# Root mean squares spread by four transposes, decay exponents formed on ACT by a relu with bias, key-value latents issued ahead of the index keys, SBUF padding of 72 instead of 88 words

## The chip, the cores and the metric

The kernel runs on one core of a Trainium2 chip. The metric is device microseconds (us) of one execution, from the median of three runs. TensorE (PE in the views) does the matrix products, VectorE (DVE) and ScalarE (ACT) the elementwise work, GpSimd (POOL) some more of it, and SyncE (SP) issues every DMA. Each engine takes its instructions in one fixed order and waits where an operand or a buffer is not ready.

## The reference, cut to what matters

One layer of a hybrid encoder on 512 tokens of 1024 channels: a layer norm, a mixing block with two branches, a layer norm, a feed-forward block with a convolution, a layer norm. The parts that the change touches:

```
# state-space branch, 32 heads in pairs, chunks of 64 tokens in the reference
a_cum = cumsum(dt * A)                        # per head
seg   = a_cum[..., :, None] - a_cum[..., None, :]
decay = exp(where(causal, seg, -inf))         # <= 1: seg is <= 0 where causal
y_diag = einsum(cb * decay, X)
v = v * rsqrt(mean(v * v over 512 channels) + eps)     # 4 groups

# attention branch
ckv   = ckv * rsqrt(mean(ckv * ckv) + eps) * kv_norm_g # 256 latent channels
k_idx = layernorm(k_idx)                               # index keys
score = sum_h relu(q_idx . k_idx) * w_idx              # selects 128 keys per query
```

The kernel works in chunks of 128 tokens. Everything is float32; the large products are split into a high and a low part in the type float32r and done as three products (high x high, low x high, high x low).

## The kernel before, in words

Activations lie with channels on the 128 partitions and 512 tokens along a row. A weight block of 128 x 1024 comes by one DMA into `wraw` (4 buffers), ACT copies it to the high part `whi` (L190), DVE subtracts to get the low part `wlo` (L191, 3 buffers each), and PE runs 24 matmuls with it (`proj`, L228, recorded at L217) into one of three PSUM accumulators `pacc`. A projection of 512 tokens thus is 24 matmuls of 512 columns.

The stages in order of time: input norm and small projections (to about 56 us), `decays` (L471), `index_keys` (L428), `latents` (L513), `scores` (L451), then the state-space part (to about 485 us): for each of four groups, `ssd_in` projects and convolves six blocks, and `ssd_core` handles one pair of heads, 16 times. In `ssd_core` the tile `G` is read back from memory (a row of cumulative decays spread over all partitions, L590), the exponent is formed by 8 DVE instructions (L623: subtract the token's own value, then the minimum with 0), ACT takes the exponential (L625), DVE multiplies by the masked products (L626), and PE uses it (L633). `ssd_norm` and `latents` call `rms_bcast` (L254): it sums squares by PE into a column per token (L259), takes the inverse root (DVE, POOL), writes it on a diagonal `dg` (DVE, L263) and spreads it over all partitions by one float32 product of 512 columns with ones (L266). After that come attention (485 to 667 us), the merge of both branches (`yahi`, `yalo` against `w_br_att`, to 709), the output projection (to 757), the feed-forward up-projection (`h1hi`, `h1lo`, to 1000) and down-projection (tiles `f`, `fw`, `fx`, `fy`, at L241).

Up to 485 us the order of instructions on each engine is made by a list scheduler from the order of the code and its own estimates of duration; from there on the order of PE is written out by hand or follows the code. Tiles live in pools. The left-hand pools (`cst`, `wrw`, `whl`, `keep`, `h1T`, `f` and others) grow from low addresses; `pad` and then `wk` are taken from the high end of a partition's memory:

```
pad = E(tc.tile_pool(name="pad", bufs=1, side="right"))
pad.tile([P, PAD], F32, name="pad")
wk = E(tc.tile_pool(name="wk", bufs=1, side="right"))
```

Nothing reads `pad`; it only moves `wk`. With 88 words `wk` begins at byte 116,352 of a partition, a multiple of 128, and so do its large tiles (`yhi`, `ylo`, `yahi`, `yalo`, `fw`, `fx`, `fy`, `wh`, `mhi`, `qi`, `G` and more). With 72 words it begins at 116,416, 64 bytes past a multiple of 128. The left-hand tiles that PE reads (`whi` and `wlo` from 24,768, `hhi` and `hlo` from 65,728, `h1hi` and `h1lo` from 49,344, the tiles `f` from 82,112, `ident` at 3,136) all begin 64 bytes past a multiple of 128.

Of the kernel before, what the change touches and what calls it, by code (L numbers as in the profile page):

```python
# [11 lines left out]
AF = mybir.ActivationFunctionType  # L12
OP = mybir.AluOpType
# [3 lines left out]
P = 128  # L17
T = 512
NT = T // P
# [17 lines left out]
OUT_STEPS = (0, 0, 0, 2, 4)  # L37
UNITS_A = [n / 18 for n in (0, 1, 1, 4, 2)]
UNITS_B = [n / 18 for n in (1, 2, 2, 5)]
PAD = 88  # L40
NOSYNC = mybir.DependencyInfo(mybir.DependencyClass.NoSync, mybir.DependencyReason.DATA)

VECS = [("ln_in_g", KD), ("ln_in_b", KD), ("kv_g", 2), ("conv_w", 96), ("conv_b", 24), ("norm_g", 16),
# [16 lines left out]
def tok(i):  # L60
    return slice(i * P, (i + 1) * P)
# [11 lines left out]
def block_kernel(ctx, tc, A, out):  # L73
    nc = tc.nc
# [15 lines left out]
    def wt(tag, shape, name, dtype=F32):  # L90
        return wk.tile(shape, dtype, name=name, tag=tag, bufs=BUFS[tag])
# [9 lines left out]
    def ct(shape, name, dtype=F32):  # L101
        return cst.tile(shape, dtype, name=name, tag=name)
# [22 lines left out]
    def flat(t):  # L125
        return t.rearrange("p a b -> p (a b)")
# [21 lines left out]
    ones = ct([P, P], "ones")  # L148
    nc.gpsimd.memset(ones, 1.0)
    ident = ct([P, P], "ident")  # L150
# [103 lines left out]
    def rms_bcast(sqs, n):  # L254

        s4 = ps("a")
        for i in range(NT):
            for j, sq in enumerate(sqs):
                nc.tensor.matmul(s4[:, i:i + 1], sq[:, tok(i)], ones[:, 0:1],  # L259
                                 start=j == 0, stop=j == len(sqs) - 1)  # L260
        r = rsqrt_small(s4[:, :NT], 1.0 / n, EPS, NT)
        dg = wt("m2", [P, NT, P], "dg")
        nc.vector.tensor_tensor(dg, ident[:, None, :].to_broadcast([P, NT, P]),  # L263
                                r[:, :, None].to_broadcast([P, NT, P]), OP.mult)
        rb = ps("b")
        nc.tensor.matmul(rb, ones, flat(dg), start=True, stop=True)  # L266
        return rb

    def stack_parts(even, odd, p, scale, cols):
# [27 lines left out]
    dt, dts, acT, cd = [kp.tile(SH, F32, name=n, tag=n) for n in ("dt", "dts", "acT", "cd")]  # L297
# [14 lines left out]
    V, S, G = "vector", "scalar", "gpsimd"  # L312
# [158 lines left out]
    def decays():  # L471
        dt4 = wt("m2", [P, 4, NT, NH], "dt4")
        u, e, s, s2 = [dt4[:, c] for c in range(4)]
        a = sp1[:, :NT * NH].rearrange("p (a b) -> p a b", a=NT)
        nc.vector.tensor_tensor(u, smt[:, :, 64:96], row["dt_bias"][:, None, :].to_broadcast(SH), OP.add)
        nc.vector.scalar_tensor_tensor(e, u, -1.0, u, OP.mult, OP.max)
        nc.scalar.activation(e, e, AF.Exp, scale=-1.0)
        nc.vector.tensor_scalar(s, e, 2.0, None, OP.add)
        nc.vector.reciprocal(s, s)
        nc.vector.tensor_tensor(s, s, e, OP.mult)  # L480
        nc.vector.tensor_tensor(s2, s, s, OP.mult)
        nc.vector.tensor_scalar(e, s2, 1.0 / 15.0, None, OP.mult)
        for c in (13, 11, 9, 7, 5, 3):
            nc.vector.scalar_tensor_tensor(e, e, 1.0 / c, s2, OP.add, OP.mult)
        nc.vector.scalar_tensor_tensor(e, e, 1.0, s, OP.add, OP.mult)
        nc.vector.tensor_scalar(u, u, 0.0, None, OP.max)
        nc.vector.scalar_tensor_tensor(dt, e, 2.0, u, OP.mult, OP.add)
        eA = sp1[:, 128:160]
        with tc.issue_after(last_pow[0].ins):
            nc.gpsimd.tensor_tensor(eA, e_t, row["A_log"], OP.pow)  # L490
        nc.vector.scalar_tensor_tensor(a, dt, -1.0, eA[:, None, :].to_broadcast(SH), OP.mult, OP.mult)
        ar = wt("m2", [NH, T], "ar")
        p = ps("c")
        for c in range(NT):
            nc.tensor.matmul(p[:NH, tok(c)], a[:, c], upper, start=True, stop=True)
        nc.scalar.activation(ar, p[:NH], AF.Copy)
        nc.sync.dma_start(ac_d, ar)
        ear = wt("m2", [NH, T], "ear")
        nc.scalar.activation(ear, ar, AF.Exp)
        nc.sync.dma_start(ea_d, ear)  # L500
        p = ps("c")
        for c in range(NT):
            nc.tensor.transpose(p[:, c * NH:(c + 1) * NH], ar[:, tok(c)], ident[:NH, :NH])
        nc.vector.tensor_copy(flat(acT), p[:, :NT * NH])
        p = ps("c")
        nc.tensor.matmul(p[:, :NT * NH], lastrow, flat(acT), start=True, stop=True)
        nc.scalar.activation(flat(cd), p[:, :NT * NH], AF.Exp)
        nc.vector.tensor_tensor(flat(u), p[:, :NT * NH], flat(acT), OP.subtract)
        nc.scalar.activation(u, u, AF.Exp)
        nc.vector.tensor_tensor(dts, dt, u, OP.mult)  # L510
# [72 lines left out]
    def ssd_core(g, j):  # L583

        s_ = sins[g]
        CT, bt, cbm, x_ = s_["CT"], s_["bt"], s_["cbm"], s_["xs"][j]
        q = 4 * g + j
        h0 = 2 * q
        G = wt("g4", [P, 2, NT, P], "G")
        nc.sync.dma_start(G.rearrange("p a c l -> p a (c l)"),  # L590
                          bass.AP(tensor=ac_d.tensor, offset=ac_d.offset + h0 * T,
                                  ap=[[0, P], [T, 2], [1, T]]))
        eaB = wt("e2", [P, T], "eaB")
        for b in range(2):
            nc.sync.dma_start(eaB[b * 64:(b + 1) * 64], bcast(ea_d[h0 + b:h0 + b + 1, :], T, 64))

        tr = v3(tr_tile())
        for c in range(NT):
            nc.tensor.transpose(tr[:, c], x_[:, tok(c)], ident)
        X4, X3 = [P, NT, 2, 64], [P, NT - 1, 2, 64]  # L600
        xd = wt("xd", X4, "xd")
        xdd = wt("xd", X3, "xdd")
        tr4 = tr.rearrange("p c (h d) -> p c h d", h=2)
        hs2 = slice(h0, h0 + 2)
        nc.vector.tensor_tensor(xdd, tr4[:, :NT - 1], dts[:, :NT - 1, hs2, None].to_broadcast(X3), OP.mult)
        nc.vector.tensor_tensor(xd, tr4, dt[:, :, hs2, None].to_broadcast(X4), OP.mult)

        sp = v3(ps("a"), NT - 1)
        for c in range(NT - 1):
            nc.tensor.matmul(sp[:, c], bt[:, c], xdd[:, c].rearrange("p h d -> p (h d)"),  # L610
                             start=True, stop=True)
        pv = wt("m2", [P, NT - 1, P], "pv")
        nc.scalar.activation(pv[:, 0], sp[:, 0], AF.Copy)
        for c in range(1, NT - 1):
            for h in range(2):
                hs = slice(h * 64, (h + 1) * 64)
                nc.vector.scalar_tensor_tensor(pv[:, c, hs], pv[:, c - 1, hs],
                                               cd[:, c, h0 + h:h0 + h + 1], sp[:, c, hs],
                                               OP.mult, OP.add)

        for h in range(2):
            for c in range(NT):
                nc.vector.tensor_scalar(G[:, h, c], G[:, h, c], acT[:, c, h0 + h:h0 + h + 1], 0.0,  # L623
                                        OP.subtract, OP.min)
        nc.scalar.activation(G, G, AF.Exp)  # L625
        nc.vector.tensor_tensor(G, G, cbm[:, None].to_broadcast([P, 2, NT, P]), OP.mult)  # L626
        yo = ps("b")
        for c in range(1, NT):
            nc.tensor.matmul(yo[:, tok(c)], pv[:, c - 1], CT[:, tok(c)], start=True, stop=True)  # L629
        yd = ps("c")  # L630
        for c in range(NT):
            for h in range(2):
                nc.tensor.matmul(yd[h * 64:(h + 1) * 64, tok(c)], xd[:, c, h], G[:, h, c],  # L633
                                 start=True, stop=True)
        v = wt("v", [P, T], "v")
        nc.vector.tensor_tensor(eaB[:, P:], yo[:, P:], eaB[:, P:], OP.mult)  # L636
        last_v[0] = nc.vector.scalar_tensor_tensor(v, x_, Dv[:, q:q + 1], yd, OP.mult, OP.add)
        nc.gpsimd.tensor_tensor(v[:, P:], v[:, P:], eaB[:, P:], OP.add)  # L638

        p = proj_h(w_("w_z", q))  # L640
        zs = wt("m2", [P, T], "zs")
        nc.scalar.activation(zs, p, AF.Tanh, scale=0.5)
        nc.vector.scalar_tensor_tensor(zs, zs, 1.0, p, OP.add, OP.mult)
        nc.gpsimd.tensor_tensor(v, v, zs, OP.mult)
        if j == 0:
            s_["ssum"] = wt("m2", [P, T], "ssum")
            s_["v"] = []
            nc.scalar.activation(s_["ssum"], v, AF.Square)
        else:
            sq = wt("m2", [P, T], "sq")  # L650
            nc.scalar.activation(sq, v, AF.Square)
            nc.gpsimd.tensor_tensor(s_["ssum"], s_["ssum"], sq, OP.add)
        s_["v"].append(v)
# [48 lines left out]
        nc.sync.dma_start(rs_d, bass.AP(tensor=rb_d.tensor, offset=rb_d.offset, ap=[[UW, AH], [0, P], [1, UW]]))  # L702

    decays()
    index_keys()
    latents()
    scores()
    sins, last_v, pins, ga = {}, [None], [], 0
    for _ in ssd_in(0):
# [177 lines left out]
    for h in range(AH + 1):  # L887
        r, hh = divmod(h, 2)
# [280 lines left out]
```

## Time and profile before

| what | value |
|---|---|
| median of 3 runs | 1130.02 us (1126.41 to 1131.23) |
| the profiled execution's own time | 1128.35 us |
| span from first to last instruction in it | 1126.3 us |
| PE busy | 1102.1 us, 98% of the span |
| PE weight loads | 902.7 us, 80% |
| DVE busy | 804.2 us, 71% |
| ACT busy | 443.0 us, 39% |
| POOL busy | 177.6 us, 16% |
| DMA | 125.59 MB, mean 112 GB/s |

Busy time of PE is the union of its instructions, which overlap each other: a matmul of 512 columns is recorded with 366 to 408 ns, but the next one starts about 227 ns after it. What a matmul costs is therefore read from start to start, or from a row of the chain of waits that merges many of them (its length divided by its count). The remaining 2.05 us between span and own time lie before and after the instructions.

### The profile page before, as it was taken

What the parts mean: (1) busy time and instruction counts of PE and PEld (TensorE: products, weight loads), DVE (VectorE), ACT (ScalarE), POOL (GpSimd) and SP (SyncE); (2) the same over time, 40 slices, a digit from 0 to 9 for tenths busy, and PEclk for the clock granted to TensorE, in tenths of its full rate; (3) what the DMA queues carried; (4) which work ended last, traced back from release to release, by engine and by line L of the source; (5) the groups of instructions that cost most, each with busy time, mean ns of one, the idle gap of its engine ahead of it and who ended that gap; (6) DMA issues with size and microseconds to landing.
All of it is one profiled execution on the core that took longest, in us unless ns stands there. A gap on an engine that the chain in (4) does not pass through costs nothing.

```text
span 1126.3 us, 14551 instructions
## 1 busy us (share of the span) xinstructions
PE 1102.1 (98%) x5410; PEld 902.7 (80%) x5410; DVE 804.2 (71%) x1542; ACT 443.0 (39%) x697; POOL 177.6 (16%) x177
## 2 busy tenths in 40 slices
PE   7999999999999999999999999999999999999996
PEld 5878787878887888878788778889888888888885
DVE  7778878857889899858989848565656565642227
ACT  5355433434432423245555524214444444432220
POOL 3000113312211232013332532040000000000002
PEclk9999999999999999999999999999999999999998
DMA  6432334273333322422222345502322222322231
GB/s 248 168 119 75 103 121 133 95 227 130 112 114 111 124 94 85 142 83 71 88 67 73 116 173 171 198 1 75 102 104 94 94 94 96 105 97 96 94 94 75
DMA packets 41638, 125.59 MB, mean 112 GB/s; under 512 B 4720, under 2 KB 9120, under 8 KB 41568
## 3 DMA queue, kind: packets, MB, share of 16 engines
q1 hardware_dynamic: 41568, 124.68, 32.7%
q8 instruction: 42, 0.69, 0.2%
q14 instruction: 28, 0.23, 0.1%
HBM read 118.21 MB, written 9.59 MB: 113 GB/s over the span
## 4 chain that ended last, share of the span: by engine, by line
PE 91%; DMA 3%; DVE 3%; ACT 1%; issue 1%; SPq 0%; DVEq 0%; ACTq 0%
PE pacc L217 56%; PE pc L217 5%; PE pacc L241 5%; PE ptr L241 4%; PE pa L217 3%; PE pb L217 3%; DMA G<-ac_d 2%; PE pc L241 2%; PE pb L241 2%; PE pa L241 2%; PE ptr L217 2%; PE pc L633 1%; PE pb L629 1%; PE pa L610 1%; PE pb L220 1%; DMA prow<-in_prow_dram 1%
## 5 line engine op out<-in xcount | busy, mean ns | idle before, releaser
L191 DVE TENSOR_TENSOR wlo<-wraw,whi 128x1024 fp32r<-128x1024 f32 x159 | 201.5, 1267 | 158.1 <-ACT whi L190 158.1
L190 ACT ACTIVATE whi<-wraw 128x1024 fp32r<-128x1024 f32 x159 | 168.2, 1058 | 265.2 <-PE pacc L217 175.2
L217 PE MATMUL pacc<-hhi,whi 128*128 128x512 f32 (+1 forms) x536 | 218.8, 408 | 3.5 <-DVE cv L550 2.5
L217 PE MATMUL pacc<-hlo,whi 128*128 128x512 f32 (+1 forms) x536 | 212.2, 396 | 0.8 <-DVE hlo L371 0.8
L217 PE MATMUL pacc<-hhi,wlo 128*128 128x512 f32 (+1 forms) x536 | 210.3, 395 | 0.0
L217 PEld LDWEIGHTS pacc<-hhi,whi 128*128 128x128 f32 (+1 forms) x536 | 101.2, 189 | 26.5 <-issue 4.2
L217 PEld LDWEIGHTS pacc<-hlo,whi 128*128 128x128 f32 (+1 forms) x536 | 100.9, 188 | 25.3 <-DVE hlo L371 3.6
L217 PEld LDWEIGHTS pacc<-hhi,wlo 128*128 128x128 f32 (+1 forms) x536 | 101.1, 189 | 19.1 <-issue 1.0
L172 POOL TENSOR_TENSOR rs_y<-rs_v,mhalf 128x1 f32<-128x1 f32 (+1 forms) x14 | 14.0, 1000 | 469.6 <-DVE rs_v L170 468.6
L217 PE MATMUL pacc<-h1hi,wlo 128*128 128x512 f32 (+1 forms) x216 | 79.0, 366 | 0.0
L217 PE MATMUL pacc<-h1hi,whi 128*128 128x512 f32 (+1 forms) x216 | 78.9, 366 | 0.0
L217 PE MATMUL pacc<-h1lo,whi 128*128 128x512 f32 (+1 forms) x216 | 78.7, 366 | 0.0
L816 POOL TENSOR_TENSOR tm<-mask,toe 128x128 f32<-128x128 f32 (+1 forms) x64 | 46.6, 731 | 135.3 <-DVE mn L827 93.5
L638 POOL TENSOR_TENSOR v<-v,eaB 128x384 f32<-128x384 f32 x16 | 23.8, 1490 | 259.2 <-DVE eaB L636 238.5
L550 DVE SCALAR_TENSOR_TENSOR cv<-pacc,cwb,cv 128x511 f32<-128x511 f32 (+2 forms) x72 | 53.3, 741 | 0.5
L217 PE MATMUL pacc<-yhi,whi 128*128 128x512 f32 x128 | 51.8, 406 | 0.0
L217 PE MATMUL pacc<-ylo,whi 128*128 128x512 f32 x128 | 50.8, 397 | 0.0
L217 PE MATMUL pacc<-yhi,wlo 128*128 128x512 f32 x128 | 50.6, 395 | 0.0
L830 ACT ACTIVATE l<-l,mn 128x128 f32<-128x128 f32 (+1 forms) x64 | 35.7, 559 | 35.1 <-DVE mn L827 33.5
L217 PEld LDWEIGHTS pacc<-h1hi,wlo 128*128 128x128 f32 x216 | 40.8, 189 | 6.6
L217 PEld LDWEIGHTS pacc<-h1hi,whi 128*128 128x128 f32 x216 | 40.7, 189 | 6.6
L217 PEld LDWEIGHTS pacc<-h1lo,whi 128*128 128x128 f32 x216 | 40.6, 188 | 6.4
(477 smaller groups left out, 2269.3 us busy)
## 6 DMA issues: line engine op xcount, KB each, us to landing
wraw<-in_w_up_dram SPq DMA_DIRECT2D x44, 512.0 KB, 3.5
wraw<-in_w_xbc_dram SPq DMA_DIRECT2D x24, 512.0 KB, 3.5
wraw<-in_w_down_dram SPq DMA_DIRECT2D x22, 512.0 KB, 3.5
wraw<-in_w_z_dram SPq DMA_DIRECT2D x16, 512.0 KB, 3.5
G<-ac_d SPq DMA_DIRECT2D x16, 512.0 KB, 4.0
wraw<-in_w_br_ssd_dram SPq DMA_DIRECT2D x16, 512.0 KB, 3.7
eaB<-ea_d SPq DMA_DIRECT2D x32, 128.0 KB, 2.9
wraw<-in_w_ga_dram SPq DMA_DIRECT2D x8, 512.0 KB, 3.5
```

The costliest lines, as they stand in the source:

```text
L172: last_pow[0] = nc.gpsimd.tensor_tensor(y, v, mhalf[:, :n], OP.pow)
L190: nc.scalar.activation(hi[:, :cols], raw[:, :cols], AF.Copy)
L191: nc.vector.tensor_tensor(lo[:, :cols], raw[:, :cols], hi[:, :cols].bitcast(F32), OP.subtract)
L217: pe(nc.tensor.matmul(p, a, b, start=start, stop=stop).ins)
L220: pe(nc.tensor.transpose(p, a, b).ins)
L241: nc.tensor.matmul(p, x[a][:, tok(i)], w[b][h], start=first and j == 0, stop=last and j == 2)
L550: nc.vector.scalar_tensor_tensor(y[:, d:], p[:, :T - d], cwb[:, 24 * k + c:24 * k + c + 1], y[:, d:], OP.mult, OP.add)
L610: nc.tensor.matmul(sp[:, c], bt[:, c], xdd[:, c].rearrange("p h d -> p (h d)"), start=True, stop=True)
L629: nc.tensor.matmul(yo[:, tok(c)], pv[:, c - 1], CT[:, tok(c)], start=True, stop=True)
L638: nc.gpsimd.tensor_tensor(v[:, P:], v[:, P:], eaB[:, P:], OP.add)
L816: nc.gpsimd.tensor_tensor(tm[:, :K - f], maskt[i][:, f:], self.toe[:, 2 * P - K + f:], OP.add)
L830: nc.scalar.activation(l[:, :K], l[:, :K], AF.Exp, bias=self.mn[:, ic], scale=-1.0, accum_out=self.sm[:, ic])
```

## The change

Four edits. In `rms_bcast` the diagonal and the product with ones go; four PE transposes, one per 128 tokens, each of the inverse root's column repeated along 128 columns, write the same spread values into the same PSUM tile. In `ssd_core` the 8 exponents of each `G` are formed on ACT as relu(a - G), with the per-token value as bias and a scale of -1, and the exponential that follows takes a scale of -1. `latents()` is called before `index_keys()`. `PAD` is 72.

```
-PAD = 88
+PAD = 72
...
         r = rsqrt_small(s4[:, :NT], 1.0 / n, EPS, NT)
-        dg = wt("m2", [P, NT, P], "dg")
-        nc.vector.tensor_tensor(dg, ident[:, None, :].to_broadcast([P, NT, P]),
-                                r[:, :, None].to_broadcast([P, NT, P]), OP.mult)
         rb = ps("b")
-        nc.tensor.matmul(rb, ones, flat(dg), start=True, stop=True)
+        for i in range(NT):
+            nc.tensor.transpose(rb[:, tok(i)], r[:, i:i + 1].to_broadcast([P, P]), ident)
         return rb
...
         for h in range(2):
             for c in range(NT):
-                nc.vector.tensor_scalar(G[:, h, c], G[:, h, c], acT[:, c, h0 + h:h0 + h + 1], 0.0,
-                                        OP.subtract, OP.min)
-        nc.scalar.activation(G, G, AF.Exp)
+                nc.scalar.activation(G[:, h, c], G[:, h, c], AF.Relu, bias=acT[:, c, h0 + h:h0 + h + 1],
+                                     scale=-1.0)
+        nc.scalar.activation(G, G, AF.Exp, scale=-1.0)
...
     decays()
+    latents()
     index_keys()
-    latents()
     scores()
```

In counts: PE loses 5 products of 512 columns and gains 20 transposes of 128; DVE loses 128 + 5 instructions; ACT gains 128; POOL and SP keep theirs. The new kernel's lines from `rms_bcast` on are 2 lower (L623 becomes L621, L625 L623, L550 L548).

The scheduler reorders much of the first 485 us. Three places.

ACT, just after the cumulative decays `ar` have been copied out of PSUM (`ear`: their exponential; `cks`: squares of the latents, which PE's sums wait for; `cv`: a convolution's first step). Before:

```order
L496 ACTIVATE ar<-pc 32x512
L190 ACTIVATE whi<-wraw 128x1024
L547 ACTIVATE cv<-pacc,cwb 128x512
L499 ACTIVATE ear<-ar 32x512
L519 ACTIVATE cks<-pacc 128x512 x2
L507 ACTIVATE cd<-pc 128x128
```

After:

```order
L494 ACTIVATE ar<-pc 32x512
L497 ACTIVATE ear<-ar 32x512
L517 ACTIVATE cks<-pacc 128x512 x2
L190 ACTIVATE whi<-wraw 128x1024
L545 ACTIVATE cv<-pacc,cwb 128x512
L505 ACTIVATE cd<-pc 128x128
L621 ACTIVATE G<-G,acT 128x128 x8
L507 ACTIVATE dt_454<-dt_454 128x128
L621 ACTIVATE G<-G,acT 128x128 x8
```

A weight split and a convolution step now stand behind the two squares instead of ahead of them, and two blocks of 8 relus follow.

DVE, at the first two pairs of heads of group 1, where the convolution `cv` of a projected block runs (three instructions on `pacc`; the last, of 509 columns, frees that accumulator for PE). Before:

```order
L191 TENSOR_TENSOR wlo<-wraw,whi 128x1024
L623 TENSOR_SCALAR G<-G,acT 128x128 x8
L550 SCALAR_TENSOR_TENSOR cv<-pacc,cwb,cv 128x511
L636 TENSOR_TENSOR eaB<-pb,eaB 128x384
L605 TENSOR_TENSOR xdd<-ptr,dts 128x384
L637 SCALAR_TENSOR_TENSOR v<-xs,Dv,pc 128x512
L606 TENSOR_TENSOR xd<-ptr,dt 128x512
L550 SCALAR_TENSOR_TENSOR cv<-pacc,cwb,cv 128x510
L626 TENSOR_TENSOR G<-G,cbm 128x1024
L623 TENSOR_SCALAR G<-G,acT 128x128 x8
L550 SCALAR_TENSOR_TENSOR cv<-pacc,cwb,cv 128x509
```

After, the same block's convolution:

```order
L191 TENSOR_TENSOR wlo<-wraw,whi 128x1024
L641 SCALAR_TENSOR_TENSOR zs<-zs,pacc 128x512
L548 SCALAR_TENSOR_TENSOR cv<-pacc,cwb,cv 128x511
L548 SCALAR_TENSOR_TENSOR cv<-pacc,cwb,cv 128x510
L548 SCALAR_TENSOR_TENSOR cv<-pacc,cwb,cv 128x509
L634 TENSOR_TENSOR eaB<-pb,eaB 128x384
```

The three convolution instructions now follow each other, with no exponents between.

PE, at the first two pairs of heads (`pa` holds the states' products, from which ACT and DVE make `pv`; `pb` uses `pv`; `pc` uses `G`). Before:

```order
L217 MATMUL pacc<-hhi,wlo 128x512
L610 MATMUL pa<-xdd,bt 128x128 x3
L217 MATMUL pacc<-hlo,whi 128x512
L217 MATMUL pacc<-hhi,whi 128x512
L217 MATMUL pacc<-hhi,wlo 128x512
L633 MATMUL pc<-G,xd 64x128 x8
L217 MATMUL pacc<-hlo,whi 128x512
```

After:

```order
L217 MATMUL pacc<-hlo,whi 128x512
L564 MATMUL ptr<-ident,bc 128x128 x4
L608 MATMUL pa<-xdd,bt 128x128 x3
L631 MATMUL pc<-G,xd 64x128 x8
L627 MATMUL pb<-bc,pv 128x128 x2
L631 MATMUL pc<-G,xd 64x128 x8
L217 MATMUL pacc<-hhi,whi 128x512
```

The product with `pv` now follows its states' products with 8 small matmuls between and no projection, and the second pair's use of `pc` follows at once.

## Rows read from the trace of the kernel before

**Rows 1.** The page: busy us (share of the span) and instructions by engine.

```profile
PE 1102.1 (98%) x5410; PEld 902.7 (80%) x5410; DVE 804.2 (71%) x1542; ACT 443.0 (39%) x697; POOL 177.6 (16%) x177
```

**Rows 2.** Waits: who for whom, us in total, times, longest.

```profile
PE pacc L217 <- DVE cv L550: 2.5, 2, 2.0
PE pa L259 <- ACT cks L519: 1.6, 1, 1.6
PE pb L629 <- DVE pv L617: 1.2, 1, 1.2
...
ACT G L625 <- DVE G L623: 23.6, 10, 3.8
```

**Rows 3.** Chain that ended last: start us, us, what, count of merged instructions.

```profile
92.72 4.54 PE pacc L217 x20
...
261.76 2.80 PE pacc L217 x12
...
292.83 0.86 PE pb L266 x2
...
298.73 0.44 PE ptr L566 x4
...
667.27 41.66 PE pacc L217 x178
...
785.06 5.44 PE pacc L217 x24
...
1016.94 2.04 PE pacc L241 x9
...
1049.77 2.06 PE pacc L241 x9
```

**Rows 4.** Timeline, 58.5 to 61.6 us: start, us, engine, line, tiles [idle before].

```profile
58.57 1.06 ACT L190 ACTIVATE whi<-wraw 128x1024 fp32r<-128x1024 f32 x1 [0.35 <-PE pacc L217]
...
59.54 0.76 ACT L547 ACTIVATE cv<-pacc,cwb 128x512 f32<-128x512 f32 x1
...
60.20 0.61 ACT L499 ACTIVATE ear<-ar 32x512 f32<-32x512 f32 x1
60.72 1.05 ACT L519 ACTIVATE cks<-pacc 128x512 f32<-128x512 f32 x2
...
61.34 0.38 PE L259 MATMUL pa<-ones,cks 128*128 128x1 f32 x2 [1.56 <-ACT cks L519]
```

**Rows 5.** Windows: us, PE, PEld, DVE, ACT, POOL busy (x), PEclk, DMA, GB/s.

```profile
62.50:66.00 3.50, 3.50 (x10) 2.70 (x9) 2.73 (x12) 1.09 (x3) 0.00 (x0) 0.51 0.93 359
130.00:445.00 315.00, 311.07 (x1653) 254.41 (x1652) 268.75 (x549) 117.51 (x167) 71.99 (x53) 1.00 0.37 123
```

**Rows 6.** Timeline of DVE, and of PE, 164.9 to 175.7 us.

```profile
164.93 1.22 DVE L191 TENSOR_TENSOR wlo<-wraw,whi 128x1024 fp32r<-128x1024 f32 x1
166.06 1.65 DVE L623 TENSOR_SCALAR G<-G,acT 128x128 f32<-128x128 f32 x8
167.63 0.75 DVE L550 SCALAR_TENSOR_TENSOR cv<-pacc,cwb,cv 128x511 f32<-128x511 f32 x1
...
172.92 2.07 DVE L623 TENSOR_SCALAR G<-G,acT 128x128 f32<-128x128 f32 x8 [0.53 <-DMA G<-ac_d]
174.90 0.74 DVE L550 SCALAR_TENSOR_TENSOR cv<-pacc,cwb,cv 128x509 f32<-128x509 f32 x1
...
175.69 0.50 PE L217 MATMUL pacc<-hhi,whi 128*128 128x512 f32 x1 [2.00 <-DVE cv L550]
```

**Rows 7.** Groups by line and form: xcount | busy, mean ns | idle.

```profile
L217 PE MATMUL pacc<-yhi,whi 128*128 128x512 f32 x128 | 51.8, 406 | 0.0
...
L830 ACT ACTIVATE l<-l,mn 128x128 f32<-128x128 f32 x16 | 6.3, 396 | 16.4 <-DVE mn L827 16.4
...
L623 DVE TENSOR_SCALAR G<-G,acT 128x128 f32<-128x128 f32 x128 | 28.8, 291 | 14.8 <-DMA G<-ac_d 14.7
```

## The prediction

> **What bounds the kernel now.** I read the busy shares first: PE is at work 98% of the span and no other engine is above 71% apart from PE's own weight loads [rows 1]. Then the waits: after the start, those of PE that the view names come to a few microseconds, 2.5 us for a convolution that frees an accumulator, 1.6 us for squares from ACT, 1.2 us for `pv` [rows 2]. ACT, on the other hand, waited 23.6 us for DVE's exponents, and nothing of that shows on PE. So the time is the number of matmuls by their start-to-start time, plus a handful of holes, and an edit is worth what it does to one of these two. The chain of waits has the start-to-start times: 20 matmuls of 512 columns on `hhi` in 4.54 us are 227 ns each, and in the up-projection 24 in 5.44 us are 227 ns too [rows 3]. That is the floor I measure against. One stretch deviates in clock: from 62.5 to 66 us the granted clock was 0.51, the lower of the two levels, 1.2 GHz; over 130 to 445 us it was 1.00 [rows 5]. Before it fell PE had had only small products and the 1.56 us hole ahead of L259 [rows 4].
>
> The sum is made against the profiled execution's own 1128.35 us (span 1126.30 and 2.05 around it), 1.67 us below the median of the runs, 1130.02. I carry each difference over to the median unchanged.
>
> **The spread of the root mean squares.** One product L266, recorded as two instructions, costs PE 0.86 us. Four transposes of 128, the same shape as the new ones, cost 0.44 us at L566 [rows 3]. Five calls: 5 x (0.44 - 0.86) = -2.1 us, on the engine that sets the end, so it counts in full. The new transposes load their weights from a column repeated 128 times, which no row shows; if that made them as dear as the old product the term would be 0, and I know no reason for more. I take -2.1. DVE loses five diagonals; they are before `rb`, which PE does not wait for, and I count nothing.
>
> **Squares ahead of a weight split.** Before, ACT ran a split (1.06), a convolution step (0.76) and the second exponential (0.61) ahead of the squares, and PE stood 1.56 us for them [rows 4]. In the new order the split and the step come behind. That is 1.82 us earlier, more than the hole: -1.6 us. What is late next is the split's weight block, needed only after the blocks split earlier (19 matmuls follow the first L259 in both orders, over 4 us), so I count nothing back. Bounds 0 to -1.6.
>
> **The clock.** The stretch at half clock lasted about 3.4 us and did half the work, a loss of 1.7 us [rows 5]. The 2.00 us hole at 175.69 [rows 6] was not followed by one. With the hole at 61 us gone, I expect the higher clock to hold: -1.7 us, bounds 0 and -1.7.
>
> **Exponents off DVE.** Before, the convolution that PE awaited at 175.69 had a block of 8 exponents ahead of its first step (1.65 us) and another ahead of its last (2.07 us, after 0.53 us for the DMA of `G`) [rows 6]. DVE is in order, so PE stood 2.00 us. In the new order the three steps follow each other: -2.0 us, bounds 0 to -2.0. DVE as a whole loses 28.8 us [rows 7]. ACT gains 128 instructions: the nearest row, a 128 x 128 exponential with a bias, has a mean of 396 ns [rows 7], so 8 take at most 3.2 us, and at least DVE's 1.65; two of ACT's instructions in a row overlap a little, and I take 2.5, or 40 us for all 16. ACT was busy 117.51 of 315 us in that stage [rows 5], so there is room. The exponents of a pair come out about 0.85 us later than on DVE. Projections on PE between a pair's `G` and its use cover that; where cover is missing see the second rival.
>
> **A new hole.** At the first two pairs PE now has only 8 products between the states' products and those with `pv`. The nearest row is the one wait of that kind before, 1.2 us [rows 2]. Queued behind it on PE are the second pair's 8 products and the next projection. I take +1.2, bounds 0 and +3.2 (a block of 8 relus in front of the copy of `pv` on ACT).
>
> **Latents ahead of index keys.** It moves their transposes and the score products some 15 us later; the same matmuls, no count changes. The score products are spread among projections in both orders. The mask is first read by the selection, hundreds of us later. The SP queue has the same transfers; `ea` is now written before the reads of `G`, behind nothing that PE awaits. 0, bounds -1 and +1.
>
> **The padding.** This edit moves no instruction, and I give it the largest term. Matmuls whose moving operand is `yhi` or `ylo` come every 2.80 us / 12 = 233 ns, those on `yahi` and `yalo` every 41.66 / 178 = 234 ns [rows 3], with weights from the same buffers as the 227 ns ones. In the down-projection a block of 9 takes 2.04 us while its other operand is a left-hand tile, and 2.06 us once it is an `fw` or `fx` in `wk`, 2.2 ns more each. In each slower case one operand starts at a multiple of 128 bytes and the other 64 bytes past one; where both start alike it is 227. After the change all of them start 64 bytes past. The terms: 128 x 3 = 384 matmuls on `y` [rows 7], 6 ns each, 2.3 us; 192 on `ya`, 7 ns, 1.3 us; ten and a half blocks of 24 in the down-projection, 2.2 ns, 0.6 us. 4.2 us, of which I take 3.9, since other matmuls of the busy stages are also a little above 227 where nothing differs in address. Bounds 0 to -5.
>
> Against this stands a rule of the Trainium skill (SBUF — State Buffer, "Who interferes with whom"): PE has two independent read ports, one for the moving operand and one for the weights, and PE never waits on anyone. By it the start address would be worth nothing. The rows disagree so far, 234 ns against 227, though they do not prove that the address is the reason.
>
> **The sum.** -2.1 - 1.6 - 1.7 - 2.0 + 1.2 + 0 - 3.9 = -10.1 us: 1118.2 on the profiled execution's scale, 1119.9 on the median's. I say 1120.
>
> **Rivals.**
> 1. The padding does nothing: the slower matmuls are slow for where their tiles lie (high or low in the partition), or for what the other engines do beside them, and moving `wk` by 64 bytes leaves them at 233. For it: the two explanations are the same in these rows, and the skill's rule above. Against: the down-projection's step from 2.04 to 2.06 comes with the operand's pool and stays for the rest of the loop. The sum without 3.9: -6.2, 1123.8.
> 2. ACT becomes the bound (the other side). Its relus stand ahead of weight splits and convolution steps in one queue. If all 16 blocks fall on PE's path, each adds the 0.85 us by which ACT is slower than DVE: 13.6 us, and -10.1 + 13.6 = +3.5, 1133.5. It turns the sign from 0.63 us a block on. For it: ACT was already waiting 23.6 us on `G`, so that chain is not slack. Against: PE shows holes at only two or three of 16 pairs before.
> 3. The holes only move: the clock falls again elsewhere and a convolution is late at another place. The sum keeps -2.1 and -3.9 alone: -6.0, 1124.0.
>
> **How the numbers follow.** A measurement of this kernel can tell 0.5%, 5.65 us, from no change: faster means below 1124.4. The forecast 0.55, rival 1 0.21, rival 3 0.15, rival 2 0.07, the rest 0.02. The forecast's own range is 1117 to 1123. Rivals 1 and 3 lie just at the 0.5% line; I count half of them as faster: 0.53 + 0.18 = 0.71. Within 0.5%: the other half and a little of the forecast and of rival 2, 0.22. Slower: 0.07. The range that holds 8 in 10 goes from 1116 (the padding's term at its bound of -5 and no new hole) to 1127 (rival 1 or 3 with some 3 us more lost, the upper bound of the new hole).
>
> **What would show it.** Chain rows of `yhi` and `yahi` at 227 ns and down-projection blocks of 2.04 throughout: the padding's term. At 233: rival 1. No window below 1.00 in clock between 12 and 1120 us, and L259 without a wait: the second and third terms. L266 at about 0.44 us for four. A wait of PE for `pv` of about 1.2 us near 125 us. If PE waits for L621, L623 or late weight splits at many pairs, rival 2; and a median above 1127 means that I mis-sized one of these.

## The result and the profile after

Five runs of each kernel: 1118.23 us in the median after (1116.49 to 1118.80), 1127.24 before (1125.81 to 1131.23). The ratio is 0.9908 with a 95% interval of 0.9889 to 0.9926: faster, by 9.0 us between the medians. The profiled execution has 1118.13 us (span 1116.4) against 1128.35 (span 1126.3) before, 10.2 less. The forecast was 1120, its range 1116 to 1127.

The page of the kernel after, busy time by engine, answers to [rows 1]:

```profile
PE 1095.8 (98%) x5420; PEld 903.8 (81%) x5420; DVE 778.2 (70%) x1409; ACT 479.8 (43%) x825; POOL 179.2 (16%) x177
```

PE has lost 6.3 us of busy time; the rest of the 9.9 us of span, 3.6, is idle time of PE. DVE lost 26.0, ACT gained 36.8; neither decides anything by itself. The waits of PE after, to be held against [rows 2]:

```profile
PE pc L217 <- DMA x<-in_x_dram: 5.7, 1, 5.7
PE pb L627 <- DVE pv L615: 1.3, 1, 1.3
PE pacc L217 <- DVE hlo L369: 1.2, 1, 1.2
...
PE pacc L217 <- DVE wlo L191: 0.7, 2, 0.5
```

The waits for a convolution (2.5 us) and for the squares (1.6 us) are gone. No row has PE waiting for `G`. A wait for `pv` of 1.3 us is there, near 126 us; the one of 1.2 us that the kernel before had at 250 us is gone, so the total for `pv` has hardly changed. The wait for `hlo`, 0.8 us before in all, is 1.2 us.

The chain after, against [rows 3] (start, us, what, count):

```profile
71.66 0.44 PE pb L264 x4
...
659.96 40.57 PE pacc L217 x178
...
1002.26 2.04 PE pacc L241 x9
...
1051.22 2.04 PE pacc L241 x9
```

Four transposes stand where a product of 0.86 us stood. The 178 matmuls on `yahi` and `yalo` take 40.57 us in place of 41.66, 227.9 ns each in place of 234. The blocks of the down-projection are 2.04 us early and late; the late ones had been 2.06.

ACT and PE around the squares, against [rows 4] (start, us, engine, what):

```profile
58.08 0.63 ACT L497 ACTIVATE ear<-ar 32x512 f32<-32x512 f32 x1
58.62 1.05 ACT L517 ACTIVATE cks<-pacc 128x512 f32<-128x512 f32 x2
59.57 1.04 ACT L190 ACTIVATE whi<-wraw 128x1024 fp32r<-128x1024 f32 x1
...
59.69 0.28 PE L259 MATMUL pa<-ones,cks 128*128 128x1 f32 x2
```

L259 follows without a wait. The windows, against [rows 5] (the last three numbers are the granted clock, the DMA share and GB/s):

```profile
17.90:21.10 3.20, 3.20 (x8) 1.89 (x8) 2.06 (x4) 3.20 (x6) 2.85 (x1) 0.50 0.41 168
62.50:66.00 3.50, 3.50 (x24) 3.19 (x23) 1.63 (x4) 2.33 (x8) 0.00 (x0) 1.00 1.06 331
```

At 62.5 us the clock is now 1.00, the higher level of 2.4 GHz. From 17.9 to 21.1 us it is 0.50, the lower one, where before it held (1.00). Ahead of that PE had stood 0.80 us for `hhi` and 1.18 us for `hlo`.

### The profile page after: what moved, and what is told of

The parts are those of the page before. It is cut to its first block, busy times and chain, and to the rows that moved or that the text cites. A ratio compares the mean times of both kernels' runs of the same rounds, so it can differ in the third digit from the quotient of the medians.

```text
span 1116.4 us, 14584 instructions
## 1 busy us (share of the span) xinstructions
PE 1095.8 (98%) x5420; PEld 903.8 (81%) x5420; DVE 778.2 (70%) x1409; ACT 479.8 (43%) x825; POOL 179.2 (16%) x177
## 4 chain that ended last, share of the span: by engine, by line
PE 91%; DVE 4%; DMA 2%; issue 1%; ACT 1%; POOL 1%; SPq 0%; DVEq 0%; ACTq 0%; POOLq 0%
PE pacc L217 56%; PE pc L217 5%; PE pacc L241 5%; PE ptr L241 4%; PE pa L217 3%; PE pb L217 3%; PE pb L241 2%; PE pa L241 2%; PE pc L241 2%; PE ptr L217 2%; PE pc L631 1%; PE pb L627 1%; DMA prow<-in_prow_dram 1%; PE pa L608 1%; PE pb L220 1%
## 5 line engine op out<-in xcount | busy, mean ns | idle before, releaser
L548 DVE SCALAR_TENSOR_TENSOR cv<-pacc,cwb,cv 128x509 f32<-128x509 f32 (+2 forms) x72 | 53.2, 741 | 0.6
L621 ACT ACTIVATE G<-G,acT 128x128 f32<-128x128 f32 x128 | 39.4, 390 | 29.0 <-DMA G<-ac_d 28.9
```

Source lines behind the costliest of these rows:

```text
L548: nc.vector.scalar_tensor_tensor(y[:, d:], p[:, :T - d], cwb[:, 24 * k + c:24 * k + c + 1], y[:, d:], OP.mult, OP.add)
L621: nc.scalar.activation(G[:, h, c], G[:, h, c], AF.Relu, bias=acT[:, c, h0 + h:h0 + h + 1], scale=-1.0)
```

## The experiments

One table first. The experiments were run in three series, each on another chip and beside runs of the kernel before; a ratio is to the kernel before of the same series, and a difference between medians of two series is less sure. "Clock" is the mean granted clock over a kernel's runs. The last column has the spans of those runs whose clock was 0.998, the highest seen. Three of these runs were profiled (PAD 8, PAD 80, index keys first), and they show no stretch at the lower level between 12 us and the last microseconds; that the others have none either is an inference.

| kernel | median us | ratio to before, 95% | clock | spans at 0.998 |
|---|---|---|---|---|
| before, first and second series | 1127.19, 1127.82 | 1 | 0.9955, 0.9956 | 1122.6 to 1123.1 |
| before, third series | 1129.90 | 1 | 0.9939 | 1122.9 |
| after | 1118.23 | 0.9908 (0.9889, 0.9926) | 0.9966 | 1114.7 |
| before, PAD 72 | 1124.76 | 0.9975 (0.9962, 0.9987) | 0.9948 | none |
| after, PAD 88 | 1122.56 | 0.9957 (0.9943, 0.9970) | 0.9967 | 1119.9 |
| after, PAD 88 and left side moved | 1122.62 | 0.9959 (0.9945, 0.9973) | 0.9968 | 1119.9, 1120.5 |
| after, PAD 8 | 1118.00 | 0.9912 (0.9896, 0.9927) | 0.9968 | 1115.3, 1116.0 |
| after, PAD 80 (third series) | 1122.26 | 0.9939 (0.9917, 0.9961) | 0.9978 | 1119.8 to 1121.2 |
| before, transposes alone | 1127.79 | 1.0004 (0.9993, 1.0015) | 0.9952 | 1123.5 |
| before, exponents on ACT alone | 1125.84 | 0.9978 (0.9966, 0.9991) | 0.9960 | 1122.4 |
| before, latents first alone | 1127.03 | 0.9993 (0.9982, 1.0004) | 0.9962 | 1123.3, 1125.2 |
| after, old product (third series) | 1118.55 | 0.9909 (0.9891, 0.9927) | 0.9973 | 1116.3 to 1116.6 |
| after, index keys first (third series) | 1119.70 | 0.9914 (0.9893, 0.9935) | 0.9962 | 1114.9, 1115.8 |
| after, exponents on DVE (third series) | 1119.50 | 0.9913 (0.9892, 0.9934) | 0.9962 | none |
| after, copies of `Dv` on POOL | 1118.47 | 0.9917 (0.9904, 0.9930) | 0.9966 | 1115.4 |

The spread of one kernel's runs follows the clock: the kernel before has spans of 1122.6 to 1123.1 us at 0.998, 1123.8 to 1126.9 at 0.996, 1127.2 to 1129.5 at 0.993, 1129.2 and 1129.4 at 0.991. A straight line through all these runs gives about 0.9 us for each 0.001 of clock. In the third series the kernel before has a lower clock (0.9939 against 0.9956) and a median some 2 us higher, so ratios of that series are some 0.002 low; there the last column is the better guide.

**Is it the address, and which?** The first two kernels change one number, so that no engine's order changes:

```
-PAD = 88        (the kernel before)
+PAD = 72
...
-PAD = 72        (the kernel after)
+PAD = 88
```

> The kernel before with PAD 72 alone; nothing else changes and every engine keeps its order. Theory A (a matmul is slower when its moving operand and its weights start at different places within 128 bytes): products on yhi, ylo, yahi and yalo come every 227 ns in place of 233, and the time falls by about 4.2 us, a ratio of 0.996 to the kernel before. Rival B (they are slow for their place high in the partition or for what runs beside them): 233 ns stays and the time stays, a ratio of 1.000.

> The kernel after with PAD set back to 88; every engine keeps its order. Theory A: the products on yhi, ylo, yahi and yalo come every 233 ns again and the time is about 4.2 us above that of the kernel after (about 1122.4, a ratio of 0.9955 to the kernel before). Rival B: 227 ns stays, and the time is that of the kernel after (1118.2, ratio 0.992).

The chain's row of the 178 matmuls on `yahi` and `yalo`, of the kernel before with PAD 72 and then of the kernel after with PAD 88:

```profile
665.48 40.57 PE pacc L217 x178
```

```profile
663.15 41.66 PE pacc L217 x178
```

The row moves with PAD alone, by 1.09 us in both kernels and in opposite ways: theory A over rival B. The price in the kernel after is 4.3 us between the medians. In the kernel before it is 2.4 to 2.8, with 4.3 at the end of its interval; these runs had a lower clock (0.9948 against 0.9955, some 0.6 us), so 4 is not excluded.

Theory A also said which difference counts. Three more kernels test it, again with every order unchanged:

```
-PAD = 72
+PAD = 88
...
-    cst = E(tc.tile_pool(name="cst", bufs=1))
+    lpad = E(tc.tile_pool(name="lpad", bufs=1)); lpad.tile([P, 16], F32, name="lpad"); cst = E(tc.tile_pool(name="cst", bufs=1))
```

> The kernel after with PAD 88 and 64 bytes of unused memory in front of the left-hand pools, so that both sides start at a multiple of 128 bytes. Theory A (only the difference between the two operands counts): 227 ns for the products on yhi, ylo, yahi and yalo, and the time of the kernel after, about 1118. Rival C (wk itself must start 64 bytes past a multiple of 128): 233 ns and about 1122.4.

```
-PAD = 72
+PAD = 8
```

> The kernel after with PAD 8: wk starts 256 bytes higher than in the kernel after, so its tiles and the left-hand ones differ by 256 in their place within 512 bytes; every engine keeps its order. So far a difference of 0 gave 227 ns for the products on yhi, ylo, yahi and yalo, 64 gave 233 and 128 gave 229 to 238. Theory F (the pattern repeats every 256 bytes): 227 ns and the time of the kernel after, 0.991 to 0.992 of the kernel before. Theory G (it repeats every 512 bytes or more): over 229 ns and about 0.9955.

```
-PAD = 72
+PAD = 80
```

> The kernel after with PAD 80: wk starts 32 bytes lower, so its tiles and the left-hand ones differ by 32 in their place within 256 bytes; every engine keeps its order. Differences of 0 and 256 gave 227 to 228 ns for the products on yhi, ylo, yahi and yalo, 64 and 128 gave 233. Theory K (any difference that is no multiple of 256 costs): above 230 ns and about 4 us more than the kernel after, 0.9955. Rival L (only differences of 64 or more do): 227 ns, 0.9915.

The same row with the left side moved, with PAD 8, with PAD 80:

```profile
660.87 41.65 PE pacc L217 x178
```

```profile
659.48 40.58 PE pacc L217 x178
```

```profile
660.94 41.67 PE pacc L217 x178
```

With the left side moved, both operands begin at a multiple of 128 bytes, and the matmuls are as slow as ever: theory A in its form "within 128 bytes" falls, and 233 ns is what rival C, a rule on the start of `wk` alone, had forecast. The down-projection tells the two apart. There the roles are turned round: the weights are `fw` or `fx` in `wk`, and the moving operand is the left-hand `whi`. Its blocks of nine, with the left side moved and with PAD 80:

```profile
1037.93 2.09 PE pacc L241 x9
```

```profile
1038.14 2.10 PE pacc L241 x9
```

With PAD 88 and the left side as it was, such a block took 2.06 us, 229 ns a matmul; with the left side moved by 64 bytes and `wk` at the same place 2.09 us, 232 ns. So the start of `wk` alone does not decide. With PAD 80 and the left side where it is in the kernel after, it took 2.10 us, 233 ns, against 2.04 and 227 there, so the start on the left alone does not decide either. Products of `hhi` with `whi`, both moved together, stayed at 227 ns.

By the starts of the pools the operands differ by 0 or 256 bytes in the fast kernels and by 32, 64 or 128 in the slow ones. So among the differences tried those that are multiples of 256 bytes are free. The others cost about 6 ns per matmul on `yahi` and `yalo` and about 5 on `yhi` and `ylo`; in the down-projection they cost 2 ns at 64 and 5 to 6 ns at 32 and 128. Why, the trace does not show. One count stays odd: with both operands in `wk` (`wh` and `mhi`), blocks of nine matmuls of the output projection took 2.04 to 2.09 us before, mostly 231 to 232 ns each, and 227 after, though their difference was 0 in both; the blocks between them read the left side, but that was not tried apart.

**The transposes.** One kernel has this edit alone on the kernel before; the other takes it back in the kernel after:

```
-        dg = wt("m2", [P, NT, P], "dg")
-        nc.vector.tensor_tensor(dg, ident[:, None, :].to_broadcast([P, NT, P]),
-                                r[:, :, None].to_broadcast([P, NT, P]), OP.mult)
         rb = ps("b")
-        nc.tensor.matmul(rb, ones, flat(dg), start=True, stop=True)
+        for i in range(NT):
+            nc.tensor.transpose(rb[:, tok(i)], r[:, i:i + 1].to_broadcast([P, P]), ident)
```

> The kernel before with the four transposes in place of diagonal and product alone. The scheduler reorders the first 485 us, but ACT still has the weight split and the convolution step ahead of the squares. Theory: PE loses 2.1 us at five places and keeps the holes before L259 (1.6 us) and before the convolution's release (2.0 us): about 1125, a ratio of 0.998. Rival: the new order alone moves the holes by more than that, and the ratio lies outside 0.996 to 1.000.

> The kernel after with the diagonal and the product with ones put back; the scheduler orders the first 485 us anew. In the profiles so far eight products with G in one piece took 1.02 us, and in two pieces 1.38; there are 24 pieces in this order against 22 in the kernel after. Theory H (the product costs 0.42 us more at each of five places, and pieces 0.35 us each): 2.1 + 0.7 = 2.8 us above the kernel after, about 1121.0, 0.994 of the kernel before. Rival I (the transposes were worth nothing in themselves): 0.7 us above it, 0.992.

Alone they are worth nothing (1.0004), though each place shows 0.44 us for 0.86, and though the wait for a convolution, which I had expected to stay at 2.0 us, is 0.8 in its profile. The rival was right that the new order takes it back, and the trace shows one way that accounts for a part. Eight products with `G` come in one piece or are broken up by others. The chain of the kernel with the transposes alone:

```profile
265.57 0.80 PE pc L631 x10
...
272.82 0.58 PE pc L631 x6
...
292.15 1.02 PE pc L631 x16
```

One piece (16 records) costs 1.02 us, two pieces 0.80 + 0.58 = 1.38. In the order of the kernel before the 16 pairs come in 20 pieces, in this one in 26, in that of the kernel after in 22. Not every cut costs the same, so I added up all pieces, each from its start to the start of what follows on PE: 17.2 us before, 19.3 with the transposes alone, 18.1 in the kernel after. The 2.1 us more are the gain of five products; for the kernel after it is 0.9. The shorter wait for the convolution (0.8 us for 2.5) should then still show, and I found nothing in the trace that takes it back: that part, 1.7 us, stays open. The test from the other side settles less: the old product back in the kernel after is 0.3 us slower between medians of different series and about 1 us at a clock of 0.998 (1116.3 to 1116.6 against 1114.7 to 1116.0 over the fast paddings), under the 2.8 of theory H and nearer to the 0.7 of rival I. The place that the new order gives the transposes has a cost of its own there: they stand right behind the root, `rs_y` from POOL, which has a product of `v` with the gate ahead of it. With the product back in, PE came to it at 197.61 us, 3.5 us after its diagonal was ready. The kernel after with PAD 88 shows the new place at its worst (POOL, then PE):

```profile
190.63 2.14 POOL L642 TENSOR_TENSOR v<-v,zs 128x512 f32<-128x512 f32 x1
192.73 1.01 POOL L172 TENSOR_TENSOR rs_y<-rs_v,mhalf 128x4 f32<-128x4 f32 x1
...
193.79 0.65 PE L264 MATMUL pb<-ident,rs_y 128*128 128x128 f32 x4 [1.70 <-POOL rs_y L172]
```

In the kernel after this hole is 0.3 us (0.52 us from one start to the next, where 0.23 is usual), none with PAD 8 and 0.7 with PAD 80; with the product it did not show.

**Latents ahead of the index keys.**

```
     decays()
-    index_keys()
     latents()
+    index_keys()
```

> The kernel before with the latents ahead of the index keys alone. The squares now stand ahead of the weight split on ACT. Theory: the hole of 1.6 us before L259 goes and with it the half clock after it (1.7 us), the wait for the convolution stays: a ratio of 0.997. Rival (the clock falls at another hole): 0.9985.

> The kernel after with the index keys ahead of the latents again. ACT has the weight split and the convolution step ahead of the squares again. Theory: the hole of 1.6 us before L259 is back, a piece more (0.35 us), the hole of 1.3 us for pv near 126 us goes: 0.7 us above the kernel after, 0.9925 of the kernel before. Rival: the order of these two calls is worth the whole hole and a stretch at half clock besides, 3.3 us, 0.9945.

Waits of PE in the kernel before with this edit alone, and in the kernel after without it:

```profile
PE pb L629 <- DVE pv L617: 2.5, 2, 2.1
PE pacc L217 <- DVE zs L643: 1.1, 1, 1.1
...
PE pa L610 <- ACT rel L463: 0.8, 1, 0.8
```

```profile
PE pa L259 <- ACT cks L517: 1.6, 1, 1.6
PE pacc L220 <- ACT x L344: 1.1, 1, 1.1
```

The hole ahead of L259 comes and goes with this edit, as both theories had it. So does the wait for `pv` near 125 us: the kernel after has it, so have its four versions with another padding and those with the old product and with `Dv` on POOL, and so have the kernel after with the exponents on DVE and the kernel before with this edit alone (0.4 us in both, beside 1.1 at 247 and 2.1 at 249); the kernel after without the edit has it not, nor has the kernel before with transposes or relus alone. DVE of the kernel after, at that place, and PE:

```profile
121.54 2.46 DVE L465 SCALAR_TENSOR_TENSOR mask<-rel,sp,mask 128x512 f32<-128x512 f32 x3 [2.57 <-ACT rel L461]
123.92 1.22 DVE L191 TENSOR_TENSOR wlo<-wraw,whi 128x1024 fp32r<-128x1024 f32 x1
125.10 0.11 DVE L466 MEMSET mask<- 64x64 f32 x1
125.13 0.68 DVE L548 SCALAR_TENSOR_TENSOR cv<-pacc,cwb,cv 128x511 f32<-128x511 f32 x1
125.73 0.46 DVE L615 SCALAR_TENSOR_TENSOR pv<-pv,cd,pa 128x64 f32<-128x64 f32 x2
...
126.25 0.49 PE L627 MATMUL pb<-bc,pv 128*128 128x128 f32 x2 [1.30 <-DVE pv L615]
```

The scores, now later, put their mask (2.46 us) and a split ahead of `pv` on DVE. In the kernel after, the edit trades a hole of 1.6 us at 60 for one of 1.3 at 126, and no net gain is clear. Alone it gave 0.9993 (0.9982 to 1.0004), so both of the ratios set down for it, 0.997 and 0.9985, were too low; the wait for the convolution, which I had expected to stay, is gone there, and waits for `pv`, `zs` and `rel` stand in its place. Without the edit the kernel after has 1114.9 and 1115.8 at a clock of 0.998, against 1114.7; but three of its six runs lie at 1118.9 to 1119.2 with a clock of 0.994 or 0.995, so its median is 1.5 us higher.

**Exponents.**

```
-                nc.vector.tensor_scalar(G[:, h, c], G[:, h, c], acT[:, c, h0 + h:h0 + h + 1], 0.0,
-                                        OP.subtract, OP.min)
-        nc.scalar.activation(G, G, AF.Exp)
+                nc.scalar.activation(G[:, h, c], G[:, h, c], AF.Relu, bias=acT[:, c, h0 + h:h0 + h + 1],
+                                     scale=-1.0)
+        nc.scalar.activation(G, G, AF.Exp, scale=-1.0)
```

> The kernel before with the exponents formed on ACT alone. Theory: the wait of 2.0 us for a convolution with exponents between its steps goes, and the hole of 1.6 us before L259 stays: about 1125, a ratio of 0.998. Rival (ACT becomes late): PE waits for exponents or weight splits at many pairs, 0.85 us each, and the ratio is above 1.000.

> The kernel after with the exponents on DVE again. Theory: exponents stand between convolution steps again and PE waits for them: 2.0 to 2.5 us above the kernel after, 0.9935 of the kernel before. Rival (with the other edits in place nothing waits for DVE): the time of the kernel after, 0.9915.

On the kernel before, the edit gives 0.9978, as the theory said: its profile has no wait for a convolution. The rival, a ratio above 1, fell. The agreement hides two more terms: the wait of 1.2 us for `pv` at 250 us is 0.3 there too, and the products with `G` come in 23 pieces, which cost 1.5 us more in all. Together that is -2.5 - 0.9 + 1.5 = -1.9 us, and the medians differ by 2.0. On the kernel after, taking it back costs 1.3 us between medians of different series, under the 2.0 to 2.5 expected. Its waits there:

```profile
PE pb L627 <- DVE pv L615: 1.5, 2, 1.1
PE pacc L217 <- DVE zs L641: 1.1, 1, 1.1
```

There is none for a convolution, with the exponents on DVE: the order had changed, and what waits is something else.

**The clock.** DVE of the kernel after copies `Dv` from a DMA that lands late, ahead of `hlo`. These are the wait of DVE and the one of PE that follows:

```profile
15.20 0.40 DVE L400 COPY Dv<-prow 64x16 f32<-64x16 f32 x2 [1.20 <-DMA prow<-in_prow_dram]
...
16.38 0.47 PE L217 MATMUL pacc<-hlo,whi 128*104 128x512 f32 x1 [1.18 <-DVE hlo L369]
```

One word moves these copies to POOL; the orders of PE, ACT and SP stay:

```
-        nc.vector.tensor_copy(Dv[hs], row["D"][hs].rearrange("p (q b) -> p b q", b=2)[:, b])
+        nc.gpsimd.tensor_copy(Dv[hs], row["D"][hs].rearrange("p (q b) -> p b q", b=2)[:, b])
```

> The kernel after with the two copies of Dv on POOL in place of DVE; the orders of PE, ACT and SP stay. In the profile of the kernel after, DVE stands 1.20 us for prow ahead of these copies, PE then stands 1.18 us for hlo, and from 17.9 to 21.1 us the granted clock is 0.5. Theory D (the wait is what makes the clock fall): the wait for hlo shrinks to about 0.5 us, the clock stays at 1.00 through the first 60 us, and the time falls by 0.7 + 1.6 = 2.3 us to about 1116. Rival E (the clock falls there or somewhere else anyway): the time falls by 0.7 us at most, and a stretch at 0.5 is still to be seen.

```profile
17.90:21.10 3.20, 2.95 (x14) 2.08 (x14) 2.50 (x5) 3.20 (x6) 3.20 (x1) 1.00 0.35 145
126.00:130.00 4.00, 3.94 (x22) 3.23 (x23) 2.96 (x7) 2.26 (x8) 0.00 (x0) 0.57 0.73 260
```

The wait for `hlo` shrinks to 0.24 us and the clock holds at 18 us, as theory D said. It then falls at 126, behind the 1.30 us for `pv`, as rival E said, and the time is the same (0.9917). In the profiles here the clock fell at 18, 62, 126, 175 and 250 us, and each time PE had stood before it, for 0.8 to 2.1 us at a time. Not each such hole had a fall behind it, and the same order has one in some profiles and none in others.

## Why the prediction was right, point by point

**The padding (-3.9).** Right, and the largest part: 4.3 us between the medians with PAD 88 and 72 in the kernel after. The rows add up to it. From the first product on `yahi` on (655 us before, 648 after) PE waits for nothing in either kernel, and there the products on `yahi` and `yalo` take 1.2 us less, the output projection 0.8, the down-projection on `wk` 0.7; matmuls on `yhi` and `ylo` come every 228.5 ns in place of 233.2, 1.8 us for 384. That is 4.5 us. My 6 ns for `y` were too many, and the output projection had no term. The Trainium skill (SBUF — State Buffer, "Who interferes with whom") says that PE has two independent read ports and waits on nobody; read as I read it, this number would be 0. The measurement, 40.57 against 41.66 us for the same 178 matmuls, decides against that reading. What was wrong is the rule behind my term: starts that agree within 128 bytes are not enough, within 256 they were. And "where both start alike it is 227" did not hold even in the kernel before, where the output projection's blocks with both operands in `wk` took 231 to 232 ns.

**The product (-2.1).** Mis-sized as a net. Per place it is right; that the pieces of the products with `G` change in number (2.1 us alone, 0.9 in the kernel after) and that the transposes come to stand right behind POOL's root was in no step of mine.

**Squares (-1.6) and the new hole (+1.2).** Both came, at 1.6 and 1.3 us. But the sum has the new hole without the old one: the wait of 1.2 us for `pv` at 250 us went, so that all waits for `pv` together moved by +0.1 and not by +1.2. And I put the hole on PE's order alone and feared relus on ACT; it belongs to the moved latents, which I had priced at 0. The failed step is "the same matmuls, no count changes": the scores' work on DVE moved too.

**The clock (-1.7).** In the profiled execution it failed: the stretch at 0.5 is at 18 in place of 62 us. Over the runs the mean clock rose from about 0.9955 to 0.9966, which at 0.9 us for each 0.001 is 1.0 us. Rival 3 was right on this term in that execution.

**Exponents (-2.0).** The wait went. That it had been due to the exponents alone is not shown: with the transposes alone it was 0.8 us, and with the latents alone, or with all edits but the relus, it was gone too. Rival 2 did not come: ACT is busy 153 us of the 315 from 130 to 445 us, and PE waits for no exponent.

**The sum.** -10.1 was expected, -9.0 measured. (The forecast stood on 1130.02 for the kernel before, the median of three runs; five have 1127.24.) At a clock of 0.998 the span goes from about 1122.8 to 1119.9 by the three other edits, and to about 1115.3 (1114.7 to 1116.0 over the fast paddings) by the padding: -2.9 and -4.6. I had -4.5 and -3.9 for these. So the time came out for a reason that was right in its largest term, with the other terms in part cancelling what I left out. That the profiled execution has 1118.13 us where the sum gives 1118.2 is luck: the padding gave more and the three other edits less than I had, and the clock fell there all the same. Singly none of the three other edits has a sure gain but the relus, and how their 2.9 us divide depends on the order that the scheduler makes of them. The changes named here (convolution, squares, the other waits, the product, pieces, the place of the transposes) add up to some -4.3 us. Two profiled executions with one stretch at 0.5 each, the kernel before and the kernel after with PAD 88, differ by 4.1; against the 2.9 of the few runs at 0.998 more than 1 us stays unassigned.

## What to carry to other kernels

When PE is busy all the time, compare start-to-start times of equal matmuls by their operands: a few nanoseconds on hundreds of matmuls were worth about as much here as the other three edits together, and one number of padding set them. Where a scheduler makes the order, price an edit by the new order's rows (who stands ahead of whom on every engine, in how many pieces a group of small products comes), not by the instruction it removes. And a hole costs more than its length when the clock falls behind it, so closing one is worth that only if no other hole takes its place.

## What was not expected of the hardware

- A matmul of 512 columns on `yahi` or `yalo` took 228 ns from start to start when the starts of its two operands' pools differed by 0 or 256 bytes and 234 when they differed by 32, 64 or 128; in the down-projection it was 227 at 0 and 256, 229 at 64 and 232 to 233 at 32 and 128.
- Eight small products broken into two pieces are dearer than in one: 0.80 + 0.58 us against 1.02.
- Between runs of one kernel the span moves with the granted clock: about 0.9 us for each 0.001 of mean granted clock (1122.6 at 0.998, 1129.2 at 0.991, before).
